# A gated unit behind the fourth gated sum, and longer stated waits in two late norms, in a hand-ordered hybrid decoder layer

## The chip, the cores and the metric

The kernel runs on one core of one Trainium2 chip. The metric is device time in microseconds (us) of one execution; lower is better. The profile comes from one profiled execution of the same program. The engines are TensorE (PE, matmuls; its weight loads are listed as PEld), VectorE (DVE), ScalarE (ACT), GpSimd (POOL) and SyncE (SP, which issues most DMAs).

## The reference

One layer with a token-mixing part and a channel part, x of 1024 tokens by 1024 channels in float32:

```python
h = rms_norm(x, g_mix_pre)
p = h @ w_in                      # RWKV inputs | S5 input u | two gates
A = rwkv7_branch(p[...])          # delta-rule state, 8 heads of 64
y = gelu(s5_scan(u))              # diagonal complex SSM, 64 states a group
B = y * sigmoid(y @ w_glu + b_glu)
m = sigmoid(gA) * (A @ w_brA) + sigmoid(gB) * (B @ w_brB)
x1 = x + rms_norm(m @ w_out, g_mix_post)
h1 = rms_norm(x1, g_ffn_pre)
z = causal_depthwise_conv3(h1 @ w_up)
out = x1 + rms_norm((gelu(z_gate) * z_val) @ w_down, g_ffn_post)
```

## The kernel before, in words

**Arithmetic.** A float32 product is made of three matmuls of split operands (high x high, low x high, high x low), at L180, L181 and L182. Three such matmuls of 128x128 by 128x512 are here called a step, and four steps (K of 512) make a tile. Each weight tile is loaded by a DMA on SP (L157), rounded to its high half on ACT (L160, wh) and its low half made on DVE (L161, wl); an activation is split by ACT L245 or L250 (high half) and DVE L246 or L251 (low half). The 1024 tokens are worked on in two halves of 512 ("half 0" and "half 1"; `th` in the code).

**What sets the order.** PE's instructions stand in the order in which the program emits them, and that order is made by hand: the stages are Python generators which issue some instructions and then yield `(cost, wait)`. `drive` (L204) keeps a model clock `now`. A generator that yields a wait is resumed once the model clock has passed it, and until then `drive` takes steps from the `fill` list, mostly steps of large matmuls. So a longer stated wait puts more of these between two instructions on PE. The instructions of DVE, ACT, POOL and SP are ordered by a scheduler, by the priority and the place at which they were emitted. On the chip each engine works through its rows in order.

**Half 0's merge** (`merge`, L1309). While the RWKV state chain of the batch runs (its PE pieces are L870 and L888, L899 and L901, L906 and L911; ACT's copies L874, L896, L903, L909; DVE's L891, L902 and the state's update L913; beside them an inverse goes on in small DVE operations, L810 and L812), the fill is:

- eight gated sums g0 to g7 (`gate`, L1278): a tile of the RWKV output by a branch weight, evicted on DVE (L1284);
- four gated units u0 to u3 (`glu_tile`, L1263) on the S5 output: a tile by w_glu, ACT's tanh (L1273), the S5 output read again by a POOL DMA (L1253) and passed through gelu (ACT L1254), DVE's gated product (L1274) and the split (ACT L250, DVE L251);
- eight merged sums s0 to s7, whose four steps need the outputs of u0 to u3 in this order, s0's last step that of u3.

The inputs of the gated units, called the S5 inputs, are four tiles loaded from memory with gelu and a split (`s5_y`, `s5_split`: L1253, L1254, L1261, L1262). Two constants of the module state where they stand in the loop: the table `XS0` the places of the S5 inputs, and `MGAP` by how many gated sums the units trail.

```python
for i in range(NK + MGAP):
    for b in XS0.get(i, ()):
        ...                       # S5 input b
    if i < NK:
        ...                       # gated sum i
    if MGAP <= i < MGAP + 4:
        ...                       # gated unit i - MGAP
```

**The late norms** (`mid_norms`, L1455, and `post_norm`, L1399). For each half the output projection is normalised, added to x and normalised again. `post_norm` applies the first norm (DVE L1417, L1418), squares (ACT) and adds the squares (DVE L278). After a stated wait, T_N2 for half 1 and T_N5 for half 0, PE sums them over the channels (`sumsq`, L264, four small matmuls into one bank). DVE makes the root of it (`rstd`: L284, then L138 to L143, "rsy"). After a wait of T_RS, PE spreads the root over the partitions (`spread`, L290), and DVE applies it: L1483 on the eight tiles of y, split into h (L245, L246). For half 0 the fill is `outproj` of half 1; for half 1 it is the conv units of half 0 (`first_units(0)`, L1528 to L1552) and `ahead` (L1513), tiles "ch" and "mm" of half 0's up-projection whose evictions are ACT's L1520. Behind half 1's norm come `prep_t` (L1489: sums and differences of the blocks of h1 for a fast product, the tiles T or "t"; DVE L1501 to L1510 with splits L245, L246), the conv units of half 1, and `fast_up`, in which PE multiplies weights (r, loaded at L1581 and L1582, combined at L1585 to L1590, split into h and l) by t; its products are L1600 to L1602, and L1636 adds a kept product ("zg").

Of the kernel before, what the change touches and what calls it, by code (L numbers as in the profile page):

```python
# [73 lines left out]
class Kern:  # L74
# [1234 lines left out]
    def merge(self, mg):  # L1309
# [7 lines left out]
        first = []  # L1317
        for i in range(NK + MGAP):
            for b in XS0.get(i, ()):
                y = self.s5_y(self.ev(s8), b, 0)  # L1320
                xs.append(self.pair(1, 4 + b))
                self.s5_split(*xs[b], y)
            if i < NK:
                first.append(self.hp[0].tile([128, 512], F32, tag=f"h{'lh'[i // 4]}{i % 4}", name=self.nm("hl"), bufs=1))
                yield from self.gate(0, i, 0, br[0:4], first[i], first[i])
            if MGAP <= i < MGAP + 4:
                m = i - MGAP
                br.append(self.pair(0, 4 + m))
# [126 lines left out]
    def mid_norms(self, th, mx):  # L1455

        nc = self.nc
        if th:
            yield 0, T_N0
            ss = self.rp()  # L1460
            self.sumsq(ss, self.acc[th], True)
            yield 0.8, 0.5
            y = self.rstd(ss, 1e-6, 1.0 / D)
            yield 0, T_RS
        else:
            yield 0, lambda: self.merged
            yield 0, T_PN
            y = self.y0
        ss = self.rp()
        yield from self.post_norm(mx, y, th, "g_mix_post", lambda k, o: self.a["x"][k * 128:k * 128 + 128, o],  # L1470
                                  lambda k, o: self.X1[k * 128:k * 128 + 128, o], squares=ss)
        y = self.rstd(ss, 1e-6, 1.0 / D)
        yield 0, T_RS
        bc = self.rp()
        self.spread(bc, y)
        yield 0.9, T_N1
        self.h[th] = [None] * NK
        for k in KORD:
            if th:
                y = self.y1[k] = self.y1p.tile([128, 512], F32, tag=f"y1{k}", name=self.nm("y1"), bufs=1)  # L1480
            else:
                y = self.tm()
            nc.vector.scalar_tensor_tensor(y, mx[k], self.vec("g_ffn_pre", k), bc, ALU.mult, ALU.mult)  # L1483
            if th == 0:
                nc.sync.dma_start(self.H0[k], y)
            self.h[th][k] = self.hsplit(y, k, self.hp[th])
        yield 0, T_N3
# [612 lines left out]
NEVA = 4  # L2100
T_KN, T_BK, T_GR, T_INV, T_LV, T_CH, T_LN, T_LF = 12.0, 10.0, 2.5, 58.0, 1.0, 0.8, 12.0, 12.0
T_X, T_GLU = 3.0, 25.0
T_N0, T_RS, T_N1, T_N2, T_N4, T_N5, T_N3 = 2.5, 4.0, 2.2, 20.0, 1.6, 24.0, 2.0
NET = 5
T_PN = 8.0
KORD = (0, 4, 1, 5, 2, 6, 3, 7)
MGAP = 3
XS0 = {1: (0, 1), 2: (2, 3)}
PACE, CREDIT = 0.8, 2.0
NLD = 10  # L2110
NWH = 4
# [81 lines left out]
```

## Time and profile before

| | |
|---|---|
| three runs | 1519.01, 1521.93 and 1526.90 us, median 1521.93 |
| the profiled execution | 1524.13 us |
| its span, first to last instruction | 1522.3 us |
| mean granted TensorE clock | 0.991 |

The span leaves 1.83 us around it. In a row of the timeline stand the start in us, the busy time in us, the engine, the line, the operation, output and inputs, sizes, and in square brackets how long the engine idled just before and what released it. Several instructions of one line can stand in one row (x3). A matmul's own duration overlaps the next one's: the starts of neighbouring matmuls tell the pace. In a row of the windows stand the stretch, its length, busy time and number of instructions for PE, PEld, DVE, ACT and POOL, the granted clock (1.00 is full), the DMA share and GB/s.

### The profile page before, as it was taken

The numbers are of one execution on the slowest core, as the hardware profiler recorded it, in microseconds if no ns is written. First come the engines' busy times: TensorE is split into PE (matmuls) and PEld (weight loads), VectorE is DVE, ScalarE is ACT, GpSimd is POOL, SyncE is SP. The second block draws the span as 40 slices with busy tenths as digits, with TensorE's granted clock in tenths as the row PEclk, the third lists the DMA queues.
The fourth block names the chain that finished last, engine by engine and source line by source line (L and its number), as shares of the span: only waits on it lengthen the run. The fifth ranks groups of instructions, "written<-read, shape, count | busy, mean of one in ns | idle before, by whom it ended". The sixth has DMA issues, their size and how long they took to land.

```text
span 1522.3 us, 23902 instructions
## 1 busy us (share of the span) xinstructions
PE 1469.8 (97%) x8804; PEld 1166.1 (77%) x8804; DVE 1158.5 (76%) x2157; ACT 726.6 (48%) x1209; POOL 180.2 (12%) x340
## 2 busy tenths in 40 slices
PE   7999999999999998999999999999999999999997
PEld 5788787787677675666788778888888887888875
DVE  7989974765655594975767888888888888698767
ACT  5465444331453434556635555555555555444451
POOL 0022111124021232030110010000000000000000
PEclk9999999999999998999999999999999999999999
DMA  6455344444332446452456575233333336944712
GB/s 211 135 154 159 98 139 145 143 135 152 107 124 96 128 120 192 146 167 70 157 189 199 182 242 180 93 108 117 113 110 117 112 109 225 333 154 138 246 59 111
DMA packets 121558, 225.26 MB, mean 148 GB/s; under 512 B 31024, under 2 KB 37168, under 8 KB 121440
## 3 DMA queue, kind: packets, MB, share of 16 engines
q1 hardware_dynamic: 90576, 154.77, 32.5%
q0 software_dynamic: 21024, 64.71, 12.9%
q10 hardware_dynamic: 9840, 4.24, 1.1%
q8 instruction: 69, 1.13, 0.3%
q14 instruction: 49, 0.40, 0.1%
HBM read 164.16 MB, written 57.41 MB: 146 GB/s over the span
## 4 chain that ended last, share of the span: by engine, by line
PE 44%; DVE 4%; DMA 4%; ACT 1%; issue 1%; SPq 0%; DVEq 0%; ACTq 0%
PE d L1779 8%; PE rp L1600 5%; PE rp L1602 5%; PE rp L1601 5%; PE mm L1602 2%; PE mm L1600 2%; PE mm L1601 2%; DMA st<-in_w_down_dram 2%; PE ch L181 1%; PE mm L180 1%; PE ch L182 1%; PE mm L181 1%; PE gm L180 1%; PE ch L180 1%; PE mm L182 1%
## 5 line engine op out<-in xcount | busy, mean ns | idle before, releaser
L180 PE MATMUL gm<-hh,wh 128*128 128x512 f32 x672 | 283.1, 421 | 1.9 <-DVE ev L1057 1.9
L181 PE MATMUL gm<-hl,wh 128*128 128x512 f32 x672 | 264.9, 394 | 0.1
L182 PE MATMUL gm<-hh,wl 128*128 128x512 f32 x672 | 264.7, 394 | 0.0
L160 ACT CAST wh<-wf 128x512 fp32r<-128x512 f32 x181 | 111.9, 619 | 171.5 <-PE gm L181 88.5
L161 DVE TENSOR_TENSOR wl<-wf,wh 128x512 fp32r<-128x512 f32 x181 | 124.3, 690 | 86.5 <-ACT wh L160 84.5
L180 PEld LDWEIGHTS gm<-hh,wh 128*128 128x128 f32 x672 | 127.0, 189 | 34.3 <-issue 4.0
L182 PEld LDWEIGHTS gm<-hh,wl 128*128 128x128 f32 x672 | 127.0, 189 | 28.1
L181 PEld LDWEIGHTS gm<-hl,wh 128*128 128x128 f32 x672 | 127.4, 190 | 22.5 <-DVE hl L246 1.0
L1779 PE MATMUL d<-xh,wl 128*128 128x512 f32 x308 | 113.5, 392 | 2.1 <-DVE wl L246 2.1
L1779 PE MATMUL d<-xh,wh 128*128 128x512 f32 x308 | 113.9, 393 | 1.1 <-DVE zg L1630 1.1
L1779 PE MATMUL d<-xl,wh 128*128 128x512 f32 x308 | 113.4, 392 | 0.6 <-DVE xl L246 0.6
L1600 PE MATMUL rp<-t,h 128*128 128x512 f32 x252 | 98.3, 390 | 1.4 <-ACT p L1614 1.4
L1602 PE MATMUL rp<-t,l 128*128 128x512 f32 x252 | 98.0, 389 | 0.0
L1601 PE MATMUL rp<-t,h 128*128 128x512 f32 x252 | 98.0, 389 | 0.0
L1779 PEld LDWEIGHTS d<-xh,wl 128*128 128x128 f32 x308 | 58.1, 189 | 15.1 <-DVE wl L246 2.9
L1779 PEld LDWEIGHTS d<-xh,wh 128*128 128x128 f32 x308 | 57.8, 189 | 14.2 <-DVE zg L1630 1.5
L246 DVE TENSOR_TENSOR l<-r,h 128x1024 fp32r<-128x1024 f32 (+1 forms) x40 | 38.9, 971 | 38.9 <-ACT h L245 38.9
L1779 PEld LDWEIGHTS d<-xl,wh 128*128 128x128 f32 x308 | 58.2, 189 | 13.2 <-DVE xl L246 0.9
L245 ACT CAST h<-r 128x1024 fp32r<-128x1024 f32 (+1 forms) x40 | 33.9, 849 | 69.5 <-PE rp L1601 67.2
L1621 DVE SCALAR_TENSOR_TENSOR y<-zv,vecs,y 128x1023 f32<-128x1023 f32 (+1 forms) x42 | 53.7, 1280 | 10.2 <-ACT y L1619 10.2
L1600 PEld LDWEIGHTS rp<-t,h 128*128 128x128 f32 x252 | 47.3, 188 | 11.9 <-ACT p L1614 2.2
L1601 PEld LDWEIGHTS rp<-t,h 128*128 128x128 f32 x252 | 47.3, 188 | 9.8
(476 smaller groups left out, 3338.1 us busy)
## 6 DMA issues: line engine op xcount, KB each, us to landing
r<-in_w_up_dram SPq DMA_DIRECT2D x42, 512.0 KB, 3.5
wf<-in_w_in_dram SPq DMA_DIRECT2D x72, 256.0 KB, 3.1
st<-in_w_down_dram SPq DMA_DIRECT2D x55, 256.0 KB, 4.3
st<-ACT SPq DMA_DIRECT2D x44, 256.0 KB, 4.2
ACT<-y POOLq DMA_DIRECT2D x21, 512.0 KB, 2.9
GT<-ev POOLq DMA_DIRECT2D x32, 256.0 KB, 3.5
wf<-in_w_br_dram SPq DMA_DIRECT2D x32, 256.0 KB, 3.4
wf<-in_w_out_dram SPq DMA_DIRECT2D x32, 256.0 KB, 2.8
```

Of the source, the lines that this page charges most:

```text
L160: self.last_wh = nc.scalar.copy(h[:, :n], f[:, :n])
L161: low = nc.vector.tensor_tensor(l[:, :n], f[:, :n], h[:, :n].bitcast(F32), ALU.subtract)
L180: mm(ps, a, xh[k], start=a0, stop=False)
L181: mm(ps, a, xl[k], start=False, stop=False)
L182: mm(ps, b, xh[k], start=False, stop=z0)
L245: a = self.nc.scalar.copy(hi, x)
L246: self.split_ops = a, (eng or self.nc.vector).tensor_tensor(lo, x, hi.bitcast(F32), ALU.subtract)
L1600: mm(ps, wh[:, c], xh, start=first and k == 0, stop=False, skip_group_check=True)
L1601: mm(ps, wh[:, c], xl, start=False, stop=False, skip_group_check=True)
L1602: mm(ps, wl[:, c], xh, start=False, stop=k == 3, skip_group_check=True)
L1621: V.scalar_tensor_tensor(y[:, lag:], z[:, 0:1024 - lag], self.vec(nme, i), y[:, lag:], ALU.mult, ALU.add)
L1779: mm(ps, w[:, c], y[:, x], start=start and k == 0, stop=stop and k == 2, skip_group_check=True)
```

## The change

Five constants, one of them a new term:

```diff
@@ mid_norms
-        yield 0, T_RS
+        yield 0, T_RS + 3.0 * th
         bc = self.rp()
         self.spread(bc, y)
@@ constants
-T_N0, T_RS, T_N1, T_N2, T_N4, T_N5, T_N3 = 2.5, 4.0, 2.2, 20.0, 1.6, 24.0, 2.0
+T_N0, T_RS, T_N1, T_N2, T_N4, T_N5, T_N3 = 2.5, 4.0, 2.2, 26.0, 1.6, 26.0, 2.0
...
-MGAP = 3
-XS0 = {1: (0, 1), 2: (2, 3)}
+MGAP = 4
+XS0 = {2: (0, 1), 3: (2, 3)}
```

The first edit is in the second root of half 1 alone (`th` is 1). No instruction is added or removed; the order of PE changes in three places, and with it the queues of the other engines.

**PE, the end of the gated units.** Before, from the last step of u3 (tile gm_6885): g7 (gm_6941) follows, then s0 (gm_6991), whose last step reads u3's output hh_6876 and hl_6877.

```order
L182 MATMUL gm_6885<-hh_6346,wl_6880 128x512
L180 MATMUL gm_6941<-hh_6050,wh_6934 128x512
...
L182 MATMUL gm_6941<-hh_6064,wl_6935 128x512
L180 MATMUL gm_6991<-hh_6563,wh_6984 128x512
...
L901 MATMUL chk_6995<-S_2614,ar_4778 64x64 x4
L180 MATMUL gm_6991<-hh_6876,wh_6984 128x512
L181 MATMUL gm_6991<-hl_6877,wh_6984 128x512
```

Now u3 (gm_6935, output hh_6926 and hl_6927) stands directly in front of s0:

```order
L182 MATMUL gm_6935<-hh_6501,wl_6930 128x512
L180 MATMUL gm_6991<-hh_6613,wh_6984 128x512
...
L901 MATMUL chk_6995<-S_2614,ar_4778 64x64 x4
L180 MATMUL gm_6991<-hh_6926,wh_6984 128x512
L181 MATMUL gm_6991<-hl_6927,wh_6984 128x512
```

Units and gated sums have changed places in pairs: where `u0 g4 u1 g5 u2 g6 u3 g7` stood, now stands `g4 u0 g5 u1 g6 u2 g7 u3`, with the state chain's pieces between the same slots as before. On ACT, DVE and POOL the S5 inputs of half 0 stand where they stood.

**DVE, the end of u3.** Before, between g7's eviction and the chain's copy L902 (UV):

```order
L1284 SCALAR_TENSOR_TENSOR hl_6933<-hl_6933,gm_6941 128x512
L161 TENSOR_TENSOR wl_7140<-wf_7141,wh_7139 128x512
L812 TENSOR_TENSOR x_6384<-x_6384,tm_6459 128x2x6x8
L1274 SCALAR_TENSOR_TENSOR ev_6878<-ev_6878,ev_6927 128x512
...
L251 SCALAR_TENSOR_TENSOR hl_6877<-ev_6878,hh_6876 128x512
L812 TENSOR_TENSOR x_6384<-x_6384,tm_6465 128x2x7x6
L902 COPY UV_5703<-chb_6996 64x128
```

Now the same copy, and u3's product and low half behind it:

```order
L902 COPY UV_5703<-chb_6996 64x128
L812 TENSOR_TENSOR x_6370<-x_6370,tm_6457 128x2x7x4
L810 TENSOR_TENSOR tm_6460<-x_6370,mt_6369 128x48
L812 TENSOR_TENSOR x_6370<-x_6370,tm_6460 128x16x3
L1274 SCALAR_TENSOR_TENSOR ev_6928<-ev_6928,ev_6975 128x512
...
L251 SCALAR_TENSOR_TENSOR hl_6927<-ev_6928,hh_6926 128x512
L1284 SCALAR_TENSOR_TENSOR ev_6983<-hl_6982,gm_6991 128x512
```

L1274 and L251 of u3 have gone from ahead of L902 to behind it; four short inverse rows lie between the two. For u0 the two stand ahead of the state's update L913, for u1 and u2 ahead of L902. Later, the transposes L835 x2 stand further forward.

**PE, half 1's sums and spread.** Before, the sums stand after the first step of tile ch_9540, the spread nine steps later, in ch_9603:

```order
L182 MATMUL ch_9540<-hh_9161,wl_9535 128x512
L264 MATMUL rp_9305<-ones_226,tm_9370 128x1 x4
L180 MATMUL ch_9540<-hh_9175,wh_9534 128x512
...
L182 MATMUL ch_9603<-hh_9175,wl_9598 128x512
L290 MATMUL rp_9610<-csts,rsy_9559 128x128 x4
L180 MATMUL ch_9603<-hh_9189,wh_9597 128x512
```

Now the sums stand in the next ch tile, ch_9584, and the spread behind an mm tile:

```order
L182 MATMUL ch_9584<-hh_9186,wl_9579 128x512
L264 MATMUL rp_9305<-ones_226,tm_9370 128x1 x4
L180 MATMUL ch_9584<-hh_9200,wh_9578 128x512
...
L182 MATMUL mm_9669<-hh_9214,wl_9664 128x512
L290 MATMUL rp_9682<-csts,rsy_9616 128x128 x4
L180 MATMUL ch_9696<-hh_9172,wh_9690 128x512
```

L264 is nine steps later and L290 fourteen steps behind it, so the spread is fourteen steps later in all; 74 steps lay between it and the first product on t (L1600) before, 60 now. Half 0's sums move likewise by three steps, with its spread at the same nine steps behind them.

## The prediction

> **What bounds the kernel now.** I read the page first: the span, the busy shares, the clock of the slices and the chain that ended last.
>
> ```profile
> span 1522.3 us, 23902 instructions
> PE 1469.8 (97%) x8804; PEld 1166.1 (77%) x8804; DVE 1158.5 (76%) x2157; ACT 726.6 (48%) x1209; POOL 180.2 (12%) x340
> PEclk9999999999999998999999999999999999999999
> PE 44%; DVE 4%; DMA 4%; ACT 1%; issue 1%; SPq 0%; DVEq 0%; ACTq 0%
> ```
>
> TensorE is busy for 97% of the span. The change neither adds nor removes a matmul, so it can only alter the 3% in which PE idles and the places where its clock is halved. The view to read next is therefore the list of PE's waits. Four of its rows lie where the change works (microseconds in all, times, longest).
>
> ```profile
> PE chk L840 <- ACT x L839: 3.8, 2, 3.4
> PE rp L264 <- DVE tm L278: 2.9, 2, 2.1
> PE rp L290 <- DVE rsy L143: 1.2, 1, 1.2
> PE chb L838 <- DVE ld L835: 1.0, 1, 1.0
> ```
>
> The L840 wait is at 586 to 590 us, in half 0's merge; ACT is busy there with the S5 inputs (L1254, L1261). L264 and L290 are the late norms' sums and the spread of their root. The windows of two microseconds show what follows the longest waits (the ninth column is the granted clock; of the five windows from 590 to 600, all at 0.50 to 0.52, the first and last stand here).
>
> ```profile
> 590.00:592.00 2.00, 2.00 (x16) 0.94 (x16) 1.80 (x4) 1.50 (x3) 1.65 (x3) 0.50 0.36 96
> 598.00:600.00 2.00, 2.00 (x6) 1.59 (x5) 0.00 (x0) 0.92 (x4) 0.00 (x0) 0.52 1.00 209
> 886.00:888.00 2.00, 2.00 (x8) 1.58 (x7) 1.69 (x6) 0.48 (x1) 0.54 (x1) 0.66 1.02 338
> 888.00:890.00 2.00, 2.00 (x7) 1.52 (x6) 1.79 (x6) 1.12 (x2) 0.54 (x1) 0.50 0.93 326
> ```
>
> Ten microseconds at half clock lose about 5.0 us of work (the L840 wait); the two windows after half 1's L264 lose 0.34 x 2 + 0.5 x 2 = 1.7 us. So a wait costs its idle time and sometimes a slow stretch behind it.
>
> **Edit 1, the merge of half 0 (MGAP, XS0).** "S5 inputs one gated sum later" does not show in the built order where it would matter: up to about 600 us the rows of ACT, DVE and POOL are those of before, so the casts that hold up L839, the 3.8 us at L840 and the 5.0 us of half clock stay. I give that part nothing. What moves is PE's order: a gated sum now stands ahead of each gated unit, and the last unit, u3, is directly in front of s0, the first merged sum, which needs u3's output in its last step. Four rows of PE give the slot times and the length of a step of three matmuls.
>
> ```profile
> 639.62 0.39 PE L182 MATMUL gm<-hh,wl 128*128 128x512 f32 x1
> ...
> 643.82 0.50 PE L180 MATMUL gm<-hh,wh 128*128 128x512 f32 x1
> 644.19 0.50 PE L181 MATMUL gm<-hl,wh 128*128 128x512 f32 x1
> ...
> 878.13 0.39 PE L180 MATMUL mm<-hh,wh 128*128 128x512 f32 x1
> ...
> 880.17 0.39 PE L180 MATMUL mm<-hh,wh 128*128 128x512 f32 x1
> ```
>
> The last two are three steps apart: 0.68 us a step. In the slots of before, u3's products now end where g7's did, at 639.62 + 0.39 = 640.0, and s0's last step wants u3's high half at 643.82 and its low half at 644.19: 4.2 us of cover. What lies between is read from u3 in before, on ACT and DVE:
>
> ```profile
> 636.13 0.68 ACT L1273 ACTIVATE ev<-gm,hb_b_glu 128x512 f32<-128x512 f32 x1
> ...
> 642.60 0.63 ACT L250 ACTIVATE hh<-ev 128x512 fp32r<-128x512 f32 x1 [1.49 <-DVE ev L1274]
> ```
>
> ```profile
> 640.05 0.69 DVE L1284 SCALAR_TENSOR_TENSOR hl<-hl,gm 128x512 f32<-128x512 f32 x1
> 640.66 0.69 DVE L161 TENSOR_TENSOR wl<-wf,wh 128x512 fp32r<-128x512 f32 x1
> ...
> 641.44 1.07 DVE L1274 SCALAR_TENSOR_TENSOR ev<-ev,ev 128x512 f32<-128x512 f32 x1
> ...
> 643.46 0.67 DVE L251 SCALAR_TENSOR_TENSOR hl<-ev,hh 128x512 fp32r<-128x512 f32 x1
> ...
> 644.22 0.27 DVE L902 COPY UV<-chb 64x128 f32<-64x128 f32 x1
> ```
>
> Bare, the four operations take 0.68 + 1.07 + 0.63 + 0.67 = 3.05 us and fit; as they ran in before they took 643.46 + 0.67 - 636.13 = 8.0 us, which would be 3.9 us too late. In the new order L1274 stands behind L902 on DVE, and L902 waits for the chain's products that PE issues just before s0's last step. In before, L902 started at 644.22 behind L251; with that gone I put it at 643.6. Then 0.27, three short operations of the inverse (0.4), L1274, L250 and L251 (2.37) give 646.7: 2.5 us after 644.19. I take **+2.5** (0 to 3.9).
>
> The units u0, u1, u2 each put a block of L1274, L161, L1284 and L251 (1.07 + 0.69 + 0.69 + 0.67 = 3.1 us) in front of an operation on which the state chain waits: L913 for u0, L902 for u1 and u2. DVE runs its queue in order, so the chain waits for the block. The chain of before shows such delays:
>
> ```profile
> 624.92 0.68 PE L906 MATMUL chk<-UV,gr 128*64 128x64 f32 x7 [0.72 <-DVE UV L902]
> ...
> 634.23 0.27 PE L888 MATMUL chk<-S,ar 64*64 64x64 f32 x2 [0.43 <-DVE S L913]
> ...
> 642.93 0.45 PE L899 MATMUL chb<-p,gr 64*64 64x64 f32 x8 [0.25 <-DVE p L891]
> ```
>
> These 1.4 us belong to the old positions and go. For the new ones I take 0.7 (the first row) for u1 and u2 and twice that, 1.5, for u0, where the state's update itself is behind the block: 2.9, net **+1.5** (-1.4 if the blocks fall in idle time, +3.1 if each costs 1.5). On DVE the transposes L835 stand earlier than before, in front of half 1's S5 inputs: the 1.0 us of L838's wait goes, **-1.0** (0 to -1.0). Edit 1: **+3.0**.
>
> **Edit 2, T_N5 24 to 26 (half 0).** L264 stands three steps later, 2.0 us, and L290 keeps its distance of nine steps.
>
> ```profile
> 835.75 1.02 PE L264 MATMUL rp<-ones,tm 128*128 128x1 f32 x8 [0.84 <-DVE tm L278]
> ...
> 850.58 0.50 PE L180 MATMUL ch<-hh,wh 128*128 128x512 f32 x1 [0.48 <-ACT hh L245]
> 851.79 0.50 PE L181 MATMUL ch<-hl,wh 128*128 128x512 f32 x1 [0.71 <-DVE hl L246]
> ```
>
> The 0.84 us wait goes, but L264 and all behind it come 2.04 - 0.84 = 1.2 us later, and the first products on h0 already waited for its halves (last two rows). PE gets there 0.84 earlier and the halves 1.2 later: a loss of **+1.2** (0, if DVE was late there for its weight splits, to +2.0).
>
> **Edit 3, T_N2 20 to 26 and T_RS + 3 (half 1).** L264 stands nine steps later, and L290 fourteen steps behind it instead of nine.
>
> ```profile
> 884.45 1.05 PE L264 MATMUL rp<-ones,tm 128*128 128x1 f32 x8 [2.05 <-DVE tm L278]
> ...
> 894.63 1.13 PE L290 MATMUL rp<-csts,rsy 128*128 128x128 f32 x8 [1.23 <-DVE rsy L143]
> ...
> 945.98 0.39 PE L1600 MATMUL rp<-t,h 128*128 128x512 f32 x1
> ```
>
> Both waits go, and with them I expect the half clock of 886 to 890: 2.05 + 1.23 + 1.7 = 5.0 us. Step by step: PE was ready for L264 at 884.45 - 2.05 = 882.4; nine steps later it is 888.5; L264 about 0.9, fourteen steps 9.5: L290 at 899.0. From L290 to the first product on t (L1600, the last row) stood 74 steps and now 60, so PE would be there at 899.0 + 0.9 + 60 x 0.68 = 940.7, 5.3 us earlier. But behind L290 hangs nearly all that DVE does for 50 us: L1483 on all of y, the halves of h1, the sums of prep_t, and last the split of the first weight pair, l.
>
> ```profile
> 895.80 2.06 DVE L1483 SCALAR_TENSOR_TENSOR y<-mx,vecs,rp 128x512 f32<-128x512 f32 x3 [1.31 <-PE rp L290]
> ...
> 932.61 0.69 DVE L246 TENSOR_TENSOR t<-tx,t 128x512 fp32r<-128x512 f32 x1 [0.69 <-ACT t L245]
> ...
> 940.47 0.69 DVE L161 TENSOR_TENSOR wl<-wf,wh 128x512 fp32r<-128x512 f32 x1 [1.40 <-ACT wh L160]
> ...
> 944.47 1.22 DVE L246 TENSOR_TENSOR l<-s,h 128x1024 fp32r<-128x1024 f32 x1
> ...
> 947.35 1.28 DVE L1636 TENSOR_TENSOR zg<-p,ch 128x512 f32<-128x512 f32 x2
> ```
>
> From 895.80 to 944.47 + 1.22 = 945.69 are 49.9 us, and PE used l at 945.98: 0.3 us of slack. In the new order four L161 of this stretch have moved ahead of L1483 (-2.8) and L1636 has come in ahead of l's split (+1.3): 48.4 us, or 46.3 without the 2.1 us of idle time in the second and third rows, which a late DVE would not have. L1483 starts at 899.0 + 1.2 = 900.2, so l is ready at 946.5 to 948.6, and PE, there at 940.7, waits. The saving turns into a wait at L1600. Against before: **+0.5** (946.5 - 945.98) to +2.6; if DVE is not what sets l, -5.3. I take +0.5, as idle time is what a late queue loses first.
>
> **Sum.** 3.0 + 1.2 + 0.5 = +4.7 us. The profiled execution took 1524.13 us, 2.2 above the median of the runs, 1521.93; so 1528.8 against it and **1526.6** against the median, 0.3% slower. A measurement of this kernel can tell about 0.5%, 7.6 us, from no change.
>
> **A rule weighed.** The trace lost 1.7 us of clock behind half 1's single wait of 2.05 us. The Trainium skill, "TensorE: Matmul & The Clock Gate", section "HAM oscillation — how this bites in real kernels", states that idle gaps of more than about 3.4 us are to be avoided, and Part 1 of the page that the clock drops after an idle activity window of that length. By that rule the new idle time at s0, an estimated 2.5 us, would leave the clock whole, and the sum stays; the trace agrees for the 3.4 us before L840 and not for the 2.05 us before L264. So I hold the drop possible below that length, as the first rival.
>
> **The rivals.**
> Half clock at s0 (slower). The new wait there is longer than the 2.05 us that was followed by 0.66 and 0.50. If u2's and s0's waits fall into one stretch of over 2 us, the clock drops, for 1.7 us of loss as at 886 or 5.0 as at 590: 1528.3 to 1531.6. Against it: steps of matmuls stand between the waits. It decides at about 2 us of idle time before s0's last step. Chance 0.25, time 1531.6.
> The saving of half 1 kept. If the weight splits, paced by PE through L160, are what DVE waits for, they come 5.3 us earlier with PE, and the T products too: 1526.6 - 5.8 = 1520.8. For it: the 1.40 us of idle time before L161. Against: DVE is dense from L1483 to 932 us. Chance 0.17.
> The S5 inputs do come later. If the emission order frees ACT before L839, 3.8 us of wait and 5.0 of half clock go: 1517.8, and with the saving of half 1 1512.0. Against: ACT's rows up to L839 are unchanged, so in this place the change does not do what its words say. Chance 0.08.
> The forecast has the remaining 0.50, with some 4 us to either side (1522.6 to 1530.6).
>
> **How the numbers follow.** Slower by over 0.5% means above 1529.5: 0.14 of the forecast's 0.50 and 0.17 of the half clock's 0.25. Faster means below 1514.3: nearly all of the third rival, 0.07, and 0.04 of the second, if edit 1 costs nothing. So faster 0.11, same 0.58, slower 0.31. The range goes from 1516 (the saving kept and edit 1 at nothing) to 1535 (half clock at s0 and the full 2.6 of edit 3).
>
> **What would show it.** Right: PE waits of 2 to 4 us on L251 at s0's last step (about 644); L840's wait and its half clock unchanged; no waits at half 1's L264 and L290, no dip at 886; a new wait of about 5 us at L1600 <- L246 near 946. Wrong: no wait at L1600 (the saving is kept), no wait at s0 (ACT and DVE reach u3 sooner than their queues say), or another clock around 590 to 600.

## The result and the profile after

The changed kernel takes 1537.86 us (median of 6 runs), the kernel before 1522.91 us beside it: a ratio of 1.0092, 95% interval 1.0071 to 1.0114. That is 11 to 17 us slower. The forecast was 4.7 us slower, inside the 0.5% that a measurement can tell; the measured time lies above the range.

The page and the cores of the profiled execution (1537.05 us; its span is 13.0 us longer than that of before):

```profile
span 1535.3 us, 23901 instructions
...
PE 1479.7 (96%) x8804; PEld 1172.0 (76%) x8804; DVE 1160.5 (76%) x2157; ACT 727.2 (47%) x1209; POOL 180.3 (12%) x340
...
core 0: 1535.3 us, clock 0.985
```

PE has the same 8804 matmuls and is busy 9.9 us longer: in this pair of executions most of the loss is not idle time but slower work. The mean clocks say the same: (1 - 0.985) x 1535.3 = 23.0 us of clock lost, against (1 - 0.991) x 1522.3 = 13.7 before; 9.3 of the 13.0 us. Over more executions the share is smaller: the six of the changed kernel have a mean clock of 0.9850, seventeen of the kernel before (those beside the first experiments) 0.9901, which is 7.9 us of clock in a difference of 15.8 us between their mean times, about half.

The list of PE's waits (microseconds, times, longest):

```profile
PE rp L1600 <- ACT h L245: 3.2, 1, 3.2
PE chk L840 <- ACT x L839: 3.2, 2, 2.7
PE rp L968 <- ACT hh L250: 2.6, 1, 2.6
PE gm L180 <- ACT hh L250: 2.6, 1, 2.6
...
PE chk L840 <- ACT gr L841: 2.0, 2, 1.7
...
PE ch L1600 <- DVE t L1533: 1.4, 1, 1.4
```

The waits at half 1's L264 and L290 and at L838 are gone from it; the wait at L840 for L839 is nearly what it was. Four are new or longer: s0's last step ("gm L180"), L968 (the transposition of the normalised chain output yn), L840 behind the copies L841, and L1600, the first product on t. In the timeline of PE:

```profile
646.28 0.51 PE L180 MATMUL gm<-hh,wh 128*128 128x512 f32 x1 [2.56 <-ACT hh L250]
647.01 0.51 PE L181 MATMUL gm<-hl,wh 128*128 128x512 f32 x1 [0.22 <-DVE hl L251]
...
671.10 1.50 PE L968 MATMUL rp<-csts,yn 128*128 128x128 f32 x8 [2.63 <-ACT hh L250]
...
688.67 0.45 PE L840 MATMUL chk<-gr,ld 32*32 32x32 f32 x16 [1.67 <-ACT gr L841]
...
896.41 0.50 PE L180 MATMUL mm<-hh,wh 128*128 128x512 f32 x1 [1.93 <-ACT t L1520]
...
953.29 0.47 PE L1600 MATMUL ch<-hh,wh 128*128 128x512 f32 x1 [1.38 <-DVE t L1533]
959.44 0.79 PE L1600 MATMUL rp<-t,h 128*128 128x512 f32 x1 [3.18 <-ACT h L245]
```

At or behind each of these places the windows of two microseconds show the clock down (two rows of each stretch, in order of time; the ninth column is the clock):

```profile
648.00:650.00 2.00, 2.00 (x19) 1.27 (x19) 1.87 (x4) 0.79 (x4) 1.19 (x2) 0.51 0.68 98
650.00:652.00 2.00, 2.00 (x6) 1.36 (x5) 0.97 (x3) 0.96 (x3) 0.04 (x1) 0.64 0.40 133
672.00:674.00 2.00, 2.00 (x7) 1.71 (x6) 2.00 (x4) 0.00 (x0) 0.00 (x0) 0.50 0.00 0
674.00:676.00 2.00, 2.00 (x7) 1.53 (x7) 0.80 (x2) 0.21 (x1) 0.00 (x0) 0.67 0.50 189
688.00:690.00 2.00, 1.33 (x18) 1.16 (x19) 1.00 (x2) 1.76 (x4) 0.54 (x1) 0.75 0.00 0
694.00:696.00 2.00, 1.98 (x12) 1.09 (x10) 1.33 (x2) 0.82 (x1) 0.00 (x0) 0.55 0.02 5
896.00:898.00 2.00, 1.59 (x5) 1.33 (x6) 1.69 (x3) 1.37 (x3) 0.88 (x2) 0.80 0.86 298
898.00:900.00 2.00, 2.00 (x6) 1.54 (x5) 1.90 (x4) 0.63 (x1) 0.20 (x1) 0.50 0.98 318
960.00:962.00 2.00, 1.96 (x5) 1.12 (x4) 2.00 (x3) 0.85 (x2) 0.00 (x0) 0.50 0.00 0
964.00:966.00 2.00, 2.00 (x8) 1.57 (x7) 0.50 (x1) 0.59 (x1) 0.00 (x0) 0.63 0.95 367
```

One minus the clock, times two, summed over a stretch, gives 1.7 us at 648, 1.7 at 672, 3.4 at 688 to 696, 1.7 at 896 and 3.4 at 958 to 966; another 1.7 is at 862 to 868, behind four short waits for h0's halves. The stretch behind L840 <- L839 is there as before, but lasts 6.8 us instead of 10.2 (it ends at 596.8) and so loses 1.7 us less, and the one at 886 is gone.

Narrow windows of 0.1 us show a regularity. In each of the fourteen traces of this case, the stretches at half clock begin a whole number of times 3.413 us apart, and each (but the one that runs into the end of the program) lasts 3.41, 6.83 or 10.24 us; so each loses 1.7, 3.4 or 5.1 us. In the changed kernel they begin, from the merge on, at 590.0, 648.0, 671.9, 689.0, 863.1, 897.2 and 958.6 us. Cut into such pieces of 3.41 us, the fourteen traces hold, from 550 to 1500 us, 37 pieces at full clock in which PE idles for 1.90 us or more, and half clock follows every one of them. It follows none in which PE idles for less than 1.1 us, and 20 of the 55 in between. Where the pieces begin differs from one execution to the next. So the same wait can fall into one piece in one execution and be divided between two in another, and a half clock seen in one profile is in part chance.

### The profile page after: what moved, and what is told of

Read it like the earlier page. It is cut to its first block, busy times and chain, and to the rows that moved or that the text cites. A ratio compares the mean times of both kernels' runs of the same rounds, so it can differ in the third digit from the quotient of the medians.

```text
span 1535.3 us, 23901 instructions
## 1 busy us (share of the span) xinstructions
PE 1479.7 (96%) x8804; PEld 1172.0 (76%) x8804; DVE 1160.5 (76%) x2157; ACT 727.2 (47%) x1209; POOL 180.3 (12%) x340
## 3 DMA queue, kind: packets, MB, share of 16 engines
q0 software_dynamic: 21024, 64.71, 12.8%
## 4 chain that ended last, share of the span: by engine, by line
PE 79%; DVE 9%; ACT 4%; DMA 4%; issue 3%; POOL 0%; SPq 0%; DVEq 0%; ACTq 0%; POOLq 0%
PE d L1779 12%; PE gm L180 10%; PE gm L181 8%; PE gm L182 8%; PE rp L1600 5%; PE rp L1602 5%; PE rp L1601 5%; PE mm L1600 2%; PE mm L1601 2%; PE mm L1602 2%; PE ch L181 2%; PE mm L180 2%; PE ch L180 2%; PE ch L182 2%; PE mm L181 1%
## 5 line engine op out<-in xcount | busy, mean ns | idle before, releaser
L180 PE MATMUL gm<-hh,wh 128*128 128x512 f32 x672 | 285.4, 425 | 4.4 <-ACT hh L250 2.6
L160 ACT CAST wh<-wf 128x512 fp32r<-128x512 f32 x181 | 112.0, 620 | 180.8 <-PE gm L181 94.7
L161 DVE TENSOR_TENSOR wl<-wf,wh 128x512 fp32r<-128x512 f32 x181 | 124.3, 690 | 88.9 <-ACT wh L160 86.1
L180 PEld LDWEIGHTS gm<-hh,wh 128*128 128x128 f32 x672 | 128.2, 191 | 37.1 <-issue 3.7
L1600 PE MATMUL rp<-t,h 128*128 128x512 f32 x252 | 99.4, 394 | 4.5 <-ACT h L245 3.2
L1621 DVE SCALAR_TENSOR_TENSOR y<-zv,vecs,y 128x1023 f32<-128x1023 f32 (+1 forms) x42 | 53.8, 1280 | 10.2 <-ACT y L1619 10.2
L1600 PEld LDWEIGHTS rp<-t,h 128*128 128x128 f32 x252 | 47.8, 190 | 15.5 <-ACT h L245 3.6
L1602 PEld LDWEIGHTS rp<-t,l 128*128 128x128 f32 x252 | 47.8, 190 | 10.6 <-DVE l L246 0.8
```

The source lines that it names most:

```text
L160: self.last_wh = nc.scalar.copy(h[:, :n], f[:, :n])
L161: low = nc.vector.tensor_tensor(l[:, :n], f[:, :n], h[:, :n].bitcast(F32), ALU.subtract)
L180: mm(ps, a, xh[k], start=a0, stop=False)
L1600: mm(ps, wh[:, c], xh, start=first and k == 0, stop=False, skip_group_check=True)
L1602: mm(ps, wl[:, c], xh, start=False, stop=k == 3, skip_group_check=True)
L1621: V.scalar_tensor_tensor(y[:, lag:], z[:, 0:1024 - lag], self.vec(nme, i), y[:, lag:], ALU.mult, ALU.add)
```

## The experiments

The time from the second row of L840 (589.94 in before) to the row of L1600 that waits for a kept product (954.98 in before) leaves out what varies at the start and the end of an execution. It is 365.0 us in before and 381.6 in the changed kernel, and it is called the measured part below. It comes from one profiled execution of each kernel, so it holds the chance of the clock; the ratios come from all runs. Ratios are to the kernel before, each with its 95% interval.

**Each edit alone.** Of edit 1, XS0 hardly counts: with XS0 alone changed, the built rows of PE, DVE, ACT and POOL are those of before, and on SP only four loads of gate tiles change places; with MGAP alone the rows of those four engines are those of the whole edit.

```diff
-MGAP = 3
-XS0 = {1: (0, 1), 2: (2, 3)}
+MGAP = 4
+XS0 = {2: (0, 1), 3: (2, 3)}
```

> The kernel before with edit 1 alone (MGAP 4, XS0 one gated sum later). Theory A (the loss is made mostly in the merge: wait of 2.6 us at s0's last step, 2.6 at L968, 1.7 at L840 <- L841, each followed by half clock): 8 to 10 us slower than before, these three waits in the trace, and no loss behind 770 us. Rival B (the loss is made mostly in half 1, edit 3): at most 3 us slower.

Measured: 1.0057 (1.0037 to 1.0077), 5.6 to 11.7 us slower; measured part 373.2, +8.2. All three waits are there, with 2.57 + 0.22, 2.64 and 1.68 us. The clock fell behind the first two but not behind the third this time: a piece ended at 693.25 us and divided that wait (692.14 to 693.82), while in the changed kernel the whole wait (687.00 to 688.67) lies in the piece that ended at 689.0. Theory A holds for the size.

```diff
-T_N0, T_RS, T_N1, T_N2, T_N4, T_N5, T_N3 = 2.5, 4.0, 2.2, 20.0, 1.6, 24.0, 2.0
+T_N0, T_RS, T_N1, T_N2, T_N4, T_N5, T_N3 = 2.5, 4.0, 2.2, 20.0, 1.6, 26.0, 2.0
```

> The kernel before with edit 2 alone (T_N5 26). Theory A: the wait of 0.84 us at L264 goes and the waits for h0's halves grow: 1 us slower than before (0 to 2). Rival: the halves were late because of weight splits on VectorE, not because of the norm: 0.8 us faster.

Measured: 1.0025 (1.0007 to 1.0042), 1 to 6 us slower; measured part 366.4, +1.3. The wait at L264 is gone; the waits for h0's halves are 0.46 + 0.39 + 0.57 + 0.78 = 2.2 us, against 0.48 + 0.71 + 0.51 = 1.7. This profile also has half clock from 849 to 856, which before has not. The rival is out. Half 1's waits have changed places as well:

```profile
876.32 0.80 PE L180 MATMUL ch<-hh,wh 128*128 128x512 f32 x1 [2.94 <-ACT t L1520]
...
894.29 1.13 PE L290 MATMUL rp<-csts,rsy 128*128 128x128 f32 x8 [3.05 <-DVE rsy L143]
```

In before they are 1.00 + 0.41 us for L1520, 2.05 at L264 (none here) and 1.23 at L290: 4.7 us, and here 6.0. This profile (1518.99 us) is the fastest of the twelve executions, so it does not show where the 1 to 6 us go.

```diff
-        yield 0, T_RS
+        yield 0, T_RS + 3.0 * th
...
-T_N0, T_RS, T_N1, T_N2, T_N4, T_N5, T_N3 = 2.5, 4.0, 2.2, 20.0, 1.6, 24.0, 2.0
+T_N0, T_RS, T_N1, T_N2, T_N4, T_N5, T_N3 = 2.5, 4.0, 2.2, 26.0, 1.6, 24.0, 2.0
```

> The kernel before with edit 3 alone (T_N2 26, T_RS + 3 for half 1). Theory A: both waits of half 1 go, and a wait of 3 to 5 us stands at the first product on t (L1600 <- L245 or L246) instead, with half clock behind it: 3 to 6 us slower than before. Rival C (that wait exists only because edit 1 has shifted the queues): 5 us faster than before, no wait at L1600.

Measured: 1.0053 (1.0035 to 1.0071), 5 to 11 us slower; measured part 371.5, +6.5. Rival C is out: the wait at L1600 is there without edit 1. In the table, the waits are the sum of PE's waits that the timeline lists in the measured part, and the half clock is what is lost to it there (all in us):

| kernel | measured part | waits | half clock |
|---|---|---|---|
| before | 365.0 | 13.8 | 6.7 |
| edit 1 alone | 373.2 | 19.4 | 10.2 |
| edit 2 alone | 366.4 | 14.6 | 7.4 |
| edit 3 alone | 371.5 | 15.3 | 11.9 |
| changed | 381.6 | 20.4 | 17.1 |

In these profiles the three edits add 8.2 + 1.3 + 6.5 = 16.0 us, against 16.5 for the whole change. That they meet so closely is partly luck, since the half clock varies between executions: 3.4 us of the half clock in edit 3's profile follow three waits for h0's halves (0.48, 0.71 and 0.51 us) that stand in before as well, without half clock behind them. By the runs the edits alone cost 0.57, 0.25 and 0.53%, 1.35% together, and the whole change 0.92%; so their losses seem to overlap. Rows of edit 3's kernel on DVE and PE show the exchange:

```profile
904.69 1.40 DVE L1483 SCALAR_TENSOR_TENSOR y<-mx,vecs,rp 128x512 f32<-128x512 f32 x2
...
945.36 0.68 DVE L1636 TENSOR_TENSOR zg<-p,ch 128x512 f32<-128x512 f32 x1
...
946.97 0.68 DVE L1585 TENSOR_TENSOR s<-r 128x512 f32<-128x512 f32 x1
...
949.50 1.22 DVE L246 TENSOR_TENSOR l<-s,h 128x1024 fp32r<-128x1024 f32 x1
```

```profile
943.36 0.47 PE L1600 MATMUL ch<-hh,wh 128*128 128x512 f32 x1 [1.18 <-DVE t L1533]
949.51 0.79 PE L1600 MATMUL rp<-t,h 128*128 128x512 f32 x1 [3.18 <-ACT h L245]
```

DVE's queue behind the spread runs nearly without a gap from L1483 to l, and l's split starts at 949.5 instead of 944.5. PE waits 4.4 us there. It gains 3.3 us at L264 and L290 and pays 4.4 and the clock behind it, down from 948 to 956.

**Edit 3 in two parts.** The wait before the sums alone, and the wait before the spread alone (the two lines above, each by itself).

> Edit 3's longer wait before the sums alone (T_N2 26): L264 nine steps later, L290 nine steps behind it. Theory A (all that counts is when the spread L290 frees VectorE's queue): the waits at L264 and L290 go, L290 comes 1 to 3 us later than before, and the first product on t waits by what PE has gained: 1 to 4 us slower than before. Rival G (only both waits together pass the slack): level within 1 us, no wait over 1 us at L1600.

Measured: 1.0011 (0.9998 to 1.0025), measured part 367.9; L290 without a wait, a wait of 1.53 + 0.53 us at the first product on t.

> Edit 3's longer wait before the spread alone (T_RS + 3): L264 keeps its place and its wait of 2 us, L290 comes five steps later. Theory A: the 1.2 us wait at L290 goes, L290 comes 2 us later than before, a wait of 1 to 3 us at L1600: 1 to 4 us slower than before. Rival G: level within 1 us, no wait over 1 us at L1600.

Measured: 1.0004 (0.9987 to 1.0021), measured part 364.0; L290 without a wait, 0.78 + 0.53 us at the first product on t. So each part alone exchanges waits for others of no larger size, and neither interval leaves out a ratio of 1. Together they cost 5 to 11 us. The mechanism of theory A is seen in each trace, its size is nearer to rival G. PE's waits in the measured part are 12.8 and 13.7 us with one part, 13.8 in before, and 15.3 with both: only both together add waiting. The rest of the cost is clock, as far as the profiles tell.

**DVE's queue in half 1.** Edit 3 alone, with eight subtractions moved to GpSimd:

```diff
-            V.tensor_tensor(b12, b22, b12, ALU.subtract)
+            self.nc.gpsimd.tensor_tensor(b12, b22, b12, ALU.subtract)
...
-            V.tensor_tensor(b21, b21, self.y1[4 + j], ALU.subtract)
+            self.nc.gpsimd.tensor_tensor(b21, b21, self.y1[4 + j], ALU.subtract)
```

> Edit 3 alone, with eight of prep_t's subtractions (L1503, L1510) on GpSimd instead of VectorE: 8 x 0.6 = 4.8 us less in VectorE's queue between the spread and the first split weights. Theory A (the wait at the first product on t is VectorE's queue): the waits at L1600 (1.2 + 3.2 us) go or fall below 1 us with their half clock; 5 to 8 us faster than edit 3 alone, level with the kernel before or up to 3 us faster. Rival (the queue is set by the weight splits or GpSimd is too slow): the waits stay within 1 us, 8 us slower than before.

Measured: 1.0051 (1.0034 to 1.0068), the same as edit 3 alone, but not for the reason that the rival names. The wait at the first product on t is gone; in its place PE waits 1.70, 2.13 and 3.46 us for weight splits, the last one before it:

```profile
940.06 0.79 PE L1602 MATMUL rp<-hh,wl 128*128 128x512 f32 x1 [3.46 <-DVE wl L161]
```

And DVE did not get the 4.8 us. Its operations grew longer wherever GpSimd's ran (rows of POOL, then of DVE):

```profile
920.14 1.69 POOL L1510 TENSOR_TENSOR tx<-tx,y 128x512 f32<-128x512 f32 x1 [0.63 <-DVE y L1504]
```

```profile
918.29 1.77 DVE L1504 TENSOR_TENSOR y<-y,tm 128x512 f32<-128x512 f32 x1 [1.18 <-POOL y L1503]
919.98 0.68 DVE L246 TENSOR_TENSOR t<-tm,t 128x512 fp32r<-128x512 f32 x1
920.59 1.79 DVE L1504 TENSOR_TENSOR y<-y,tm 128x512 f32<-128x512 f32 x1
```

L1504 takes 0.68 us in before. Two of the three waits name DVE's split L161, the first ACT's L160. The experiment does not show what a shorter queue of DVE would bring.

**What the merge's new waits come from.** First, the changed kernel with u3 ahead of g7:

```diff
+            if i == NK - 1:
+                br.append(self.pair(0, 4 + i - MGAP))
+                yield from self.glu_tile(i - MGAP, xs, self.ev(), lambda: self.s5_y(self.ev(s8), i - MGAP, 0), br[4 + i - MGAP])
             if i < NK:
...
-            if MGAP <= i < MGAP + 4:
+            if MGAP <= i < NK - 1:
```

> The changed kernel with its last pair exchanged: u3 ahead of g7, so that g7's twelve matmuls lie between u3 and s0 again. Theory A: the wait at s0's last step and the 1.3 us of half clock behind it go, 4 us faster than the changed kernel; the waits at L968 and at L840 <- L841 stay, as they come from other places in the queues. Rival D: these two follow from the wait at s0 and go as well: 9 us faster than the changed kernel.

Measured: 1.0074 (1.0049 to 1.0098). From L840's second row to L840's last batch (679.51, 0.49 us of wait) are 93.9 us, against 98.6 in the changed kernel and 90.3 in before. The waits at L968 and L841 are gone, as rival D has it, but s0's went elsewhere, to the chain:

```profile
641.27 0.45 PE L899 MATMUL chb<-p,gr 64*64 64x64 f32 x8 [2.72 <-DVE p L891]
```

```profile
639.04 0.69 DVE L161 TENSOR_TENSOR wl<-wf,wh 128x512 fp32r<-128x512 f32 x1 [2.44 <-ACT wh L160]
639.82 1.03 DVE L1274 SCALAR_TENSOR_TENSOR ev<-ev,ev 128x512 f32<-128x512 f32 x1
640.93 0.29 DVE L891 TENSOR_TENSOR p<-p,chk 128x128 f32<-128x128 f32 x1
```

L891, on the chain, stands behind u3's L1274. In this order the transposes L835 are back at their old place, so this run leaves open whether they or s0's wait cause the two later waits. One order edge tells them apart:

```diff
+            if not spare and getattr(self, "normed", None) is not None:
+                self.tc.add_manual_dep(self.levelled.ins, self.normed.ins.name, ORDER)
```

Here `levelled` is a transpose L835 and `normed` the latest product L960.

> The changed kernel with one order edge: the last batch's transposes L835 on VectorE come behind the product yn (L960) again, as they did in the kernel before. Theory E (both late waits of the merge, 2.6 us at L968 and 1.7 at L840 <- L841, with the half clock behind each, come from the transposes' new place, not from the wait at s0): both go, 8 us faster than the changed kernel, that is 6 us slower than before; s0's wait of 2.6 us stays. Rival: only L968's goes, 4 us.

Measured: 1.0053 (1.0034 to 1.0072), measured part 375.6, 6.0 us shorter than the changed kernel's. s0 waits 2.57 + 0.22 us as there, L968 not at all, and the wait for L841 is gone. Theory E holds. The rows of DVE tell how, first in before:

```profile
663.19 1.29 DVE L960 TENSOR_TENSOR yn<-yn,rsy 128x512 f32<-128x512 f32 x2
664.40 0.68 DVE L1284 SCALAR_TENSOR_TENSOR ev<-hl,gm 128x512 f32<-128x512 f32 x1
...
666.86 0.69 DVE L835 STREAM_TRANSPOSE ld<-gr 32x512 f32<-32x512 f32 x1
```

and in the changed kernel:

```profile
665.09 1.41 DVE L835 STREAM_TRANSPOSE ld<-gr 32x512 f32<-32x512 f32 x2
...
668.47 0.68 DVE L1284 SCALAR_TENSOR_TENSOR ev<-hl,gm 128x512 f32<-128x512 f32 x1
...
669.67 0.68 DVE L1289 TENSOR_TENSOR ev<-ev,hl 128x512 f32<-128x512 f32 x1
670.27 1.28 DVE L960 TENSOR_TENSOR yn<-yn,rsy 128x512 f32<-128x512 f32 x2
```

With L835 forward, the chain of the root behind it and then L960 come after the whole eviction of the next merged sum. L968 needs L960's yn, first ready at about 670.9; the row of PE names L250, which ended at the same time. The copies L841 come late on ACT, behind two S5 inputs of half 1 (changed kernel; in before both copies stand ahead of the first L1254):

```profile
684.20 1.15 ACT L1254 ACTIVATE et<-et 128x512 f32<-128x512 f32 x2
685.26 2.07 ACT L1261 CAST e<-et 128x512 fp32r<-128x512 f32 x2
...
687.88 0.74 ACT L841 COPY gr<-chk 32x256 f32<-32x256 f32 x2
```

With the edge, the copies stand ahead of them again. Last, more cover at s0:

```diff
-        for m in range(NK):
+        yield from self.skewed_sums(mg, br[4:8], first)
+        for m in range(2, NK):
...
+        for ps, w, _, _, _, _ in parts:
+            yield from self.mm3_steps(ps, w, 0, xh, xl, [0, 1, 2], last=False)
+        for ps, w, to, t, g, f in parts:
+            yield from self.mm3_steps(ps, w, 0, xh, xl, [3], first=False)
```

> The changed kernel with the first two merged sums skewed: three steps of s0, three of s1, then the last step of each, so that three more steps (2.0 us) lie between u3 and the first use of its output. Theory A (s0's wait is missing cover): the wait of 2.56 + 0.22 us falls to 0.7 or less and the half clock at 648 to 652 goes, 3 to 4 us faster than the changed kernel. Rival F (the wait is VectorE's queue and goes elsewhere, as with the exchanged pair): a wait of 2 us or more on a state chain piece nearby, no gain.

Measured: 1.0059 (1.0037 to 1.0082), measured part 381.1. The wait at s0 is gone, and one of 2.09 us stands at L899 for L891 instead, with half clock behind it at 657.9: rival F in the trace (of the slowest of the six executions). The ratio's interval overlaps the changed kernel's, so a gain is not shown.

**The S5 inputs really later.** XS0 moves no row of PE, DVE, ACT or POOL, so an order edge was put in, on the kernel before (with the edge for L835, which keeps the last batch in order and by itself moves no row of the kernel before; `lev` is the last copy L839):

```diff
+        if th == 0:
+            self.tc.add_manual_dep(y.ins, self.lev.ins.name, ORDER)
...
-XS0 = {1: (0, 1), 2: (2, 3)}
+XS0 = {3: (0, 1, 2, 3)}
```

> The kernel before with the S5 inputs of half 0 really later: an order edge puts gelu L1254 behind the level's copies L839 on ScalarE (XS0 at 3, which by itself moves nothing), with the edge of the transposes that keeps the last batch in order. Theory (the wait of 3.4 + 0.4 us at L840 is ScalarE held by the S5 inputs): the wait goes, and its ten microseconds of half clock: 8 us faster than before. Rival (u0 and the chain then wait for the S5 inputs instead): at most 3 us faster, with a new wait at u0's first step.

Measured: 1516.12 us, 0.9952 (0.9935 to 0.9969): 5 to 10 us faster than the kernel before, and the lowest ratio of all. The wait for L839 is gone; two others of 1.39 and 2.25 us stand in its place, with 6.8 and 3.4 us of half clock behind them, together as long as the 10.2 us of before:

```profile
587.60 0.47 PE L842 MATMUL chk<-gr,x 32*32 32x32 f32 x16 [1.39 <-ACT gr L843]
...
618.85 0.59 PE L903 MATMUL chb<-p,gr 64*64 64x64 f32 x6 [2.25 <-DVE p L895]
```

(Lines here are two to four higher than in before: L842 is L840, the second triangular product of the level, whose copies are L839 and L841; L903 is the chain's L899.) So the saving that the theory names is not in this trace: from L792, ahead of the level (535.44 us in before, 533.39 here), to L968 (664.33 and, as L972, 661.10) it is only 1.2 us shorter. The gain is in the runs: their mean clock is 0.9908 against 0.9875, which is 5.1 of the 6.8 us between the mean times. Which slow stretches the other executions are spared is not shown. Two ways to go on, the first with the second pair behind the last copy L841 (`lev2`):

```diff
-            self.tc.add_manual_dep(y.ins, self.lev.ins.name, ORDER)
+            self.tc.add_manual_dep(y.ins, (self.lev2 if b > 1 else self.lev).ins.name, ORDER)
```

> As the kernel with the S5 inputs behind L839, but with the second pair of them behind the level's second copies (gr, there L843) as well, which waited for the casts there (1.39 us at the second triangular product, and half clock from 588 to 596). Theory: that wait and its clock go too: 10 to 12 us faster than the kernel before. Rival: u0, whose last steps read the second pair, waits for it instead, or the half clock comes anyway: 7 us faster as with the first pair alone, or less.

Measured: 0.9962 (0.9944 to 0.9979). No wait is left in the level and the clock holds until 598, but the chain's first piece (L894; L888 in before) waits 1.79 us for a copy on ACT, and the clock falls behind it: no better than the kernel above.

> As the kernel with the S5 inputs behind L839, but all four of them behind the level's second copies. Theory: no wait in the level at all, and no half clock there, but u0 stands 8 to 10 us behind the last copy while gelu and casts of four inputs take 7 us of ScalarE: a wait of 0 to 2 us at u0, 8 to 12 us faster than the kernel before. Rival: u0's wait is longer and brings the half clock back: 5 us faster or less.

Measured (all four behind the last L841): 1.0043 (1.0026 to 1.0059), 4 to 9 us slower than before. The loss goes beyond the rival, and its largest wait is not u0's: the chain's first piece (here L891) waits 5.55 us for L877, the copy L874 of before, on ACT; u0 waits 1.67 + 0.64, and the clock falls four times from 597 to 638.

## Why the prediction was wrong, point by point

**S5 inputs.** Right that their edit does nothing: the wait at L840 stayed (2.74 + 0.42 us, against 3.42 + 0.41), and half clock behind it.

**s0.** "I take +2.5" was right: 2.56 + 0.22 us, from the queue that was described, L902, then L1274, L250 and L251 (rows of DVE, then of ACT, in the changed kernel). The upper bound of 3.9 is 3.8 by its own figures (8.0 - 4.2), and nothing hangs on it.

```profile
643.74 0.28 DVE L902 COPY UV<-chb 64x128 f32<-64x128 f32 x1
...
644.55 1.02 DVE L1274 SCALAR_TENSOR_TENSOR ev<-ev,ev 128x512 f32<-128x512 f32 x1
...
646.26 0.69 DVE L251 SCALAR_TENSOR_TENSOR hl<-ev,hh 128x512 fp32r<-128x512 f32 x1
```

```profile
645.60 0.63 ACT L250 ACTIVATE hh<-ev 128x512 fp32r<-128x512 f32 x1 [1.28 <-DVE ev L1274]
```

**The chain's blocks.** Forecast 2.9 us, net +1.5; the chain's waits there are 0.86, 0.34, 0.39 and 0.83 us, 2.4 in all, net +1.0. Right in kind, and in size as a sum; u0's share was 0.86 us, not 1.5.

**"-1.0 (0 to -1.0)" for L835.** This step failed. The 1.0 us wait at L838 did go, but what moved back when L835 moved forward was not asked: L960, on which L968 hangs, and the copies L841 behind the S5 inputs of half 1 on ACT. With the edge that puts L835 back, the measured part is 6.0 us shorter (two waits, 4.3 us in the changed kernel, and 5.1 us of half clock less; some smaller waits come back). The term was -1.0 and is about +5. Its bounds held no loss at all.

**The clock.** The sum gave no clock to any new wait; the rival gave it one place, with a chance of 0.25. It came at s0, as that rival has it (1.7 us), and at five further places. This step failed too, and it is the largest miss: 9.3 of 13.0 us in the profiled pair, about half of the difference over the runs. In the words of the prediction "a wait costs its idle time and sometimes a slow stretch behind it": behind the three waits of 1.67, 2.63 and 3.18 us it cost 3.4, 1.7 and 3.4 us. The price comes in steps of 1.7 us, and it was due for every piece of 3.41 us that held 1.90 us or more of idle time.

**Edit 2.** Forecast +1.2 us, interval of the run 1 to 6; the trace shows 0.84 us gone and 0.5 more for the halves, less than the +2.0 behind the forecast. That the number fits is therefore luck. What the trace has besides, 1.3 us more of waits in half 1 and another stretch of half clock, is not tied to the edit by any run; the cause of the larger part is open.

**Edit 3.** The mechanism was right: the removed waits come back as a wait at L1600 for DVE's queue, and the rival that the saving is kept is out. The size was not: +0.5 forecast, with 2.6 as the upper end; alone it is 5 to 11 us. l was ready at 949.50 + 1.22 = 950.7 us, 2.1 behind the upper end of 946.5 to 948.6. The length of DVE's queue was right: 46.0 us from the first L1483 (904.69) to l, forecast 46.3. Its start was the term that failed: 904.7 us instead of 900.2. The spread came at 902.8 us instead of 899.0 (a wait of 1.82 us for L1520 and a stretch of half clock from 853 to 860 lay on the way), and half clock behind the wait cost another 3.4 us.

The Trainium skill ("TensorE: Matmul & The Clock Gate", Part 1) has the clock drop after an idle window of about 3.4 us. The runs differ from it: a piece of 3.41 us need not be idle throughout, as half clock followed every piece with 1.90 us or more of idle time, and single waits of 1.67, 2.6 and 3.2 us. The same page says that the window is free-running and the effect varies from run to run; that agrees with the pieces of 3.41 us in the traces, and with L840's wait of 1.67 us, which was followed by half clock in the changed kernel and not, at 1.68 us, with edit 1 alone.

Open: what decides for a piece with 1.1 to 1.9 us of idle time, and what share of edit 2's loss is more than clock. Whether a shorter queue of DVE would bring half 1's saving was not shown, since GpSimd's help lengthened DVE's own work.

## What to carry to other kernels

A wait that is taken from PE by issuing it later is only gained if the engine that feeds PE next has slack; ask what hangs on the later instruction before counting the gain, and price the wait that comes back with the clock behind it, in steps of 1.7 us. One profile is not enough to price it, since the half clock differs between executions of one kernel; compare mean clocks over runs. When an instruction moves forward in a queue, list what it passes: each operation behind it is late by its length plus whatever now fits in front. Where a constant does not move a row in the built order, an order edge does; here it gave the kernel with the lowest ratio (0.9952).

## What the runs showed of the hardware

- In each of fourteen traces the stretches at half clock began a whole number of times 3.413 us apart and lasted 3.41, 6.83 or 10.24 us. They followed every piece of 3.41 us at full clock with 1.90 us or more of PE idle time (37 of 37 from 550 to 1500 us), and none with less than 1.1 us. In between, half clock followed a wait of 1.39 us once (S5 inputs behind L839) and did not follow one of 1.66 us (T_RS + 3 alone).
- The mean clock of 0.985 against 0.991 in the two profiles stands for 9.3 us; over runs, 0.985 against 0.990, for 7.9 us.
- An elementwise operation of two inputs on DVE took 1.79 us instead of 0.68 while GpSimd ran one (1.69 us); in four such pairs the DVE operation ended 0.55 us after GpSimd's. The Trainium skill, "GPSIMD Engine Reference", section "Specifications", says that GpSimd's interface is shared with VectorE and that instructions with two SBUF inputs contend; the trace agrees.
